# Where tiles lie in memory: gaps ahead of the feed-forward and turned-output tiles of a four-layer decoder trunk

## The chip, the cores and the metric

The kernel runs on one core of a Trainium2 chip. The core has five engines that run side by side, each with its own queue of instructions: TensorE (PE; its weight loads are shown apart as PEld), VectorE (DVE), ScalarE (ACT), GpSimd (POOL) and SyncE (SP), which here only issues DMAs. Data that the engines work on lies in a memory of 128 partitions, the same byte range in every partition; "byte 182784" below is an address within a partition. TensorE multiplies a stationary operand, which a weight load brings into the array, by a moving operand, which streams past it.

The metric is the time of one execution on the device, in microseconds, as the median of several runs.

## The reference

A decoder trunk of four layers on 256 positions of width 1024, in float32. Each layer is a token mixer and a feed-forward block, each followed by a layer norm of `ALPHA * x + h`. Layers 0 and 3 mix with HGRN2 (a gated linear recurrence), layer 1 with mLSTM, layer 2 with an S5 state space.

```python
for i in range(DEPTH):
    kind = i % N_MIXERS
    if kind == 0:
        h = _hgrn2_mixer(x, ...)
    elif kind == 1:
        h = _mlstm_mixer(x, ...)
    else:
        h = _s5_mixer(x, ...)
    x = _layernorm(ALPHA * x + h, ln_g[i, 0], ln_b[i, 0])
    x = _layernorm(ALPHA * x + _swiglu(x, ffn_w_gate_up[i], ffn_w_down[i]), ln_g[i, 1], ln_b[i, 1])

def _swiglu(x, w_gate_up, w_down):
    gate, up = jnp.split(x @ w_gate_up, 2, axis=-1)
    return (jax.nn.silu(gate) * up) @ w_down
```

The hidden width of the feed-forward block is 2816. The HGRN and mLSTM mixers end with a product of the mixed values and a 1024 x 1024 weight.

## The kernel before

**Products of split numbers.** TensorE multiplies operands of type float32r, whose mantissa is short. So that the result is as exact as float32, each operand is split in two: `hi` is the value rounded to float32r (ScalarE, line 151), `lo` is what is left (VectorE, line 152). A product is then three matmuls, hi by hi, lo by hi and hi by lo (`mm3`, lines 182 to 184, and for the last block of a layer the loop of line 374). `ws_wide` (lines 212 and 215) does the same with two matmuls for 512 and 256 columns.

**Weights.** All weights come from HBM in pieces of 1 MB (128 partitions of 2048 floats), in the order of one list that `plan` makes. SP issues the loads, three stage buffers ahead; ScalarE and VectorE split each piece into `hi` and `lo` tiles of 1024 floats, of which there are eight each. All of these, and the activations `xx`, lie at multiples of 512 bytes.

**The feed-forward block** (`ffn`, line 299) walks over 11 blocks of 256 hidden columns. For blocks 2 to 9, `across` computes gate and up with the weights as the stationary operand (64 matmuls a block, lines 212 and 215), adds the parts into `sum` tiles, applies silu, multiplies, and splits the result into `hh` and `hl` (`parts`, lines 344 and 345). Blocks 0, 1 and 10 are computed the other way round and turned (line 339) before they are split. `dproj` then adds the block's share of the down projection: here `hh` and `hl` are the stationary operands, 128 columns at a time, and the moving operands are 512 columns of the split down weights. A block's `dproj` is 2 halves of the block x 2 halves of the positions x 2 halves of the output x 3 = 24 matmuls. In the steady part of a layer, `across` of one block and `dproj` of the one before follow each other.

**The output projection** (`out_proj`) of the HGRN and mLSTM layers works in the same way: `transposed` allocates two tiles `oh` and `ol` of 8192 bytes for the turned and split output of the mixer; these are the stationary operands, and the moving ones are the split weights. It is 96 matmuls of 512 columns a layer, or four times 24.

**S5 preparation.** VectorE work for layer 2's tables is spread over the feed-forward blocks of layers 0 and 1.

**Where tiles lie.** Tiles come from pools. A pool's tiles are laid one behind the other in the order of their first allocation, and a pool is put behind those that are open at that time; when it closes, the next one takes its place. A tile that comes to lie on an older one waits until the older one is released (`reuse_waits="tile"`). So the size of a tile that is never used shifts all tiles of the pool that follow it. The kernel before does this at three places: `GAPS` (line 33) gives the bytes of a tile `gap` which `ffn` allocates ahead of all others (lines 304 to 306); one column of it is set by a memset on POOL, so that the allocation has a writer. Layer 3 has no such tile.

The tiles of `ffn` are 1024 bytes each (`sg`, `hd`, `hh`, `hl`, `sum`) and those of `transposed` 8192, so all tiles of one kind and layer have the same offset past a multiple of 512. Before the change this is:

| tiles | pool position where the gap or tile starts | gap, bytes | first tile behind it | offset past a multiple of 512 |
|---|---|---|---|---|
| `ffn`, layer 0 | 182752 | 32 | 182784 | 0 |
| `ffn`, layer 1 | 181568 | 256 | 181824 | 64 |
| `ffn`, layer 2 | 145600 | 448 | 146048 | 128 |
| `ffn`, layer 3 | 145600 | none | 145600 | 192 |
| `oh`, `ol`, layers 0 and 3 | 153280 | none | 153280 | 192 |
| `oh`, `ol`, layer 1 | 149696 | none | 149696 | 192 |

In the HGRN layers the pool also holds the mask and three score tiles `att` ahead of `oh`, and behind it `v`, the gates `g`, and in a second pool behind the first the keys, queries and decay tiles of the score loop (lines 640 to 700). In the mLSTM layer nearly all of its tiles lie behind `ol`.

Of the kernel before, what the change touches and what calls it, by code (L numbers as in the profile page):

```python
# [9 lines left out]
F32 = mybir.dt.float32  # L10
# [7 lines left out]
P = 128  # L18
# [11 lines left out]
BIG = 1e30  # L30
AHEAD = 1
ROWS = (0, 1, NBLK - 1)
GAPS = (32, 256, 448)


class Trunk:
# [262 lines left out]
    def ffn(self, i, gb, out=None, perm=False, rev=False, extra=()):  # L299
        nc, tc = self.nc, self.tc  # L300
        with tc.tile_pool(name=self.uid("ffn"), bufs=2, reuse_waits="tile") as fp:
            down = [[self.bank("a") for _ in range(2)] for _ in range(2)]

            if i < len(GAPS):
                gap = fp.tile([P, GAPS[i] // 4], F32, name=self.uid("gap"), bufs=1)
                nc.gpsimd.memset(gap[:, 0:1], 0.0)
            hid, gu, dn, turned, wide = {}, {}, {}, {}, {}
            self.table("silu_and_others")
            extra = list(extra)
# [114 lines left out]
            for h in range(2):  # L424
                self.layernorm(h, down[h], gb, out, perm, rev)

    def transposed(self, pool):

        return tuple(pool.tile([P, KD, S], F32R, name=self.uid(n)) for n in ("oh", "ol"))

    def out_proj(self, key, gb, ot, turn):
# [934 lines left out]
def plan(layers, ffn):  # L1366

    p = []
    for i in layers:
        j = i // 3  # L1370
        if i % 3 == 0:
            p += [("w_hg", j, s) for s in (0, 1, 8, 9, 10, 11, 4, 5, 6, 7, 2, 3, 12, 13, 14, 15)] + [("w_ho", j, s) for s in range(4)]
        elif i % 3 == 1:
            p += [("w_ml", s) for s in range(4)] + [("ml_gw",)] + [("w_ml", s) for s in range(4, 12)] + [("w_mo", s) for s in range(4)]
        else:
            p += [("w_si", s) for s in range(4)] + [("w_so", s) for s in (0, 1, 2, 4, 5, 3, 6, 7)]
        if ffn:
            gu = lambda b: [("w_gu", i, b, 0), ("w_gu", i, b, 1)]
            dn = lambda b: [("w_dn", i, b)]
            p += gu(0) + gu(1) + dn(0)  # L1380
            for b in range(2, NBLK):
                p += gu(b) + dn(b - 1)
            p += dn(NBLK - 1)
    return p


def trunk(tc, aps, out, layers=range(DEPTH), ffn=True):
    with ExitStack() as ctx:
        t = Trunk(ctx, tc, aps)
        nc = tc.nc  # L1390
        layers = list(layers)
        t.plan = plan(layers, ffn)
        with tc.tile_pool(name="first", bufs=1, reuse_waits="tile") as fp:
            t.warm_up(fp)
# [127 lines left out]
```

## Time and profile before

| | |
|---|---|
| median of 3 runs | 1251.75 us (1250.62 to 1251.87) |
| profiled execution | 1251.88 us |
| its span, first to last instruction | 1250.1 us |
| mean granted TensorE clock | 0.997 |
| HBM read | 233.94 MB |

The profile is of one execution. It gives each engine's busy time, the groups of instructions by line with their mean durations, the waits, and the order of time. Two things help in reading it here. A matmul's duration in a row (some 390 ns for 512 columns) is longer than the distance to the next matmul, because one begins while the one before still drains; so a rate is read from the time of many matmuls in a row, not from the mean duration. And rows name tiles as out<-in, moving operand first: `a<-hi,hh` is a matmul into bank `a` that moves `hi` past the stationary `hh`.

### The profile page before, as it was taken

To read this page: it belongs to the slowest core of one execution; us is meant where nothing else is said; L and a number is where in the kernel's file an instruction comes from. 1 tells how busy PE (TensorE), PEld (TensorE's weight loads), DVE (VectorE), ACT (ScalarE), POOL (GpSimd) and SP (SyncE) were. 2 spreads that over 40 slices of the span, in tenths; PEclk is the share of its full clock that TensorE was granted. 3 is DMA by queue.
4 is the path that set the end of the run, shared out by engine and by line. 5 is a ranking of instruction groups with operands and counts; after the bars stand their busy time and mean duration, and the time that the engine had idled before them with its cause. 6 is when DMAs were issued, how large, how long until landed. Compare 5 with 4: busy or idle time off the path is not lost.

```text
span 1250.1 us, 21400 instructions
## 1 busy us (share of the span) xinstructions
PE 1230.6 (98%) x8464; PEld 1031.6 (83%) x8464; DVE 956.2 (76%) x1717; ACT 694.3 (56%) x1126; POOL 34.8 (3%) x63
## 2 busy tenths in 40 slices
PE   9999999999999999999999999999999999999997
PEld 8977888888798888888877788888889878888886
DVE  6887889796887799887699696666486887766664
ACT  7755575565477555555544355555359654555551
POOL 0000000000100000000000000000000000000000
PEclk9999999999999999999999999999999999999999
DMA  8733476666373288667565456555446432755540
GB/s 325 290 137 135 150 267 236 219 220 225 121 274 129 102 305 307 234 235 247 209 217 210 165 202 231 191 181 201 169 173 219 157 134 102 270 184 186 194 143 34
DMA packets 50245, 247.91 MB, mean 198 GB/s; under 512 B 6337, under 2 KB 15953, under 8 KB 23777
## 3 DMA queue, kind: packets, MB, share of 16 engines
q1 hardware_dynamic: 50016, 246.46, 55.0%
q8 instruction: 66, 1.08, 0.3%
q14 instruction: 35, 0.28, 0.1%
q0 software_dynamic: 128, 0.09, 0.0%
HBM read 233.94 MB, written 12.58 MB: 197 GB/s over the span
## 4 chain that ended last, share of the span: by engine, by line
PE 88%; DVE 6%; DMA 2%; ACT 2%; issue 1%; POOL 0%; SPq 0%; DVEq 0%; ACTq 0%; POOLq 0%
PE g L212 18%; PE g L182 10%; PE g L184 10%; PE g L183 9%; PE g L215 9%; PE a L183 8%; PE a L182 8%; PE a L184 8%; DVE lo L152 2%; PE a L374 1%; PE t L273 1%; DMA bc<-in_s_bc 1%; PE a L668 1%; DMA w<-in_w_gu 1%; PE a L548 1%
## 5 line engine op out<-in xcount | busy, mean ns | idle before, releaser
L152 DVE TENSOR_TENSOR lo<-w,hi 128x1024 fp32r<-128x1024 f32 x388 | 470.3, 1219 | 117.6 <-ACT hi L151 107.6
L151 ACT CAST hi<-w 128x1024 fp32r<-128x1024 f32 x388 | 405.3, 1051 | 186.5 <-PE a L183 98.0
L212 PE MATMUL g<-xx,hi 128*128 128x512 f32 x1024 | 356.6, 397 | 0.5 <-DVE sum L356 0.4
L215 PE MATMUL g<-xx,lo 128*128 128x256 f32 x1024 | 264.6, 279 | 0.0
L212 PEld LDWEIGHTS g<-xx,hi 128*128 128x128 f32 x1024 | 185.8, 188 | 37.5 <-DVE sum L356 1.2
L215 PEld LDWEIGHTS g<-xx,lo 128*128 128x128 f32 x1024 | 193.0, 188 | 10.8
L182 PE MATMUL g<-hi,xx 128*128 128x512 f32 (+1 forms) x416 | 166.5, 401 | 2.4 <-ACT xx L292 2.1
L184 PE MATMUL g<-lo,xx 128*128 128x512 f32 (+1 forms) x416 | 163.7, 395 | 0.0
L183 PE MATMUL g<-hi,xx 128*128 128x512 f32 (+1 forms) x416 | 163.4, 394 | 0.0
L183 PE MATMUL a<-hi,hl 128*128 128x512 f32 x328 | 129.3, 394 | 1.0 <-DVE hl L345 1.0
L182 PE MATMUL a<-hi,hh 128*128 128x512 f32 x328 | 129.0, 394 | 0.1
L184 PE MATMUL a<-lo,hh 128*128 128x512 f32 x328 | 129.0, 393 | 0.0
L355 ACT COPY sum<-g 128x256 f32<-128x256 f32 x128 | 47.7, 373 | 139.7 <-PE g L212 139.5
L356 DVE TENSOR_TENSOR sum<-g,sum 128x256 f32<-128x256 f32 x128 | 53.9, 421 | 61.9 <-ACT sum L355 61.5
L182 PEld LDWEIGHTS g<-hi,xx 128*128 128x128 f32 x416 | 78.4, 189 | 19.3 <-ACT xx L292 3.5
L184 PEld LDWEIGHTS g<-lo,xx 128*128 128x128 f32 x416 | 78.2, 188 | 16.4 <-DVE lo L152 0.4
L183 PEld LDWEIGHTS g<-hi,xx 128*128 128x128 f32 x416 | 78.4, 188 | 14.6
L183 PEld LDWEIGHTS a<-hi,hl 128*128 128x128 f32 x328 | 61.6, 188 | 15.6 <-DVE hl L345 1.8
L184 PEld LDWEIGHTS a<-lo,hh 128*128 128x128 f32 x328 | 61.6, 188 | 13.6
L182 PEld LDWEIGHTS a<-hi,hh 128*128 128x128 f32 x328 | 61.5, 188 | 13.3 <-ACT hh L344 0.9
L182 PE MATMUL g<-xx,hi 128*128 128x256 f32 x192 | 54.5, 284 | 0.0
L184 PE MATMUL g<-xx,hi 128*128 128x256 f32 x192 | 54.4, 283 | 0.0
(308 smaller groups left out, 1734.9 us busy)
## 6 DMA issues: line engine op xcount, KB each, us to landing
w<-in_w_gu SPq DMA_DIRECT2D x88, 1024.0 KB
w<-in_w_dn SPq DMA_DIRECT2D x44, 1024.0 KB
w<-in_w_hg SPq DMA_DIRECT2D x30, 1024.0 KB
w<-in_w_ml SPq DMA_DIRECT2D x12, 1024.0 KB
gb<-in_ln SPq DMA_DIRECT2D x8, 1024.0 KB
w<-in_w_ho SPq DMA_DIRECT2D x8, 1024.0 KB
w<-in_w_so SPq DMA_DIRECT2D x8, 1024.0 KB
w<-in_w_mo SPq DMA_DIRECT2D x4, 1024.0 KB
```

What stands on the lines that cost most here:

```text
L151: self.nc.scalar.copy(hi, x)
L152: i = self.nc.vector.tensor_tensor(lo, x, hi.bitcast(F32), ALU.subtract).ins
L182: mm(ps, lh, rh, start=start, stop=False)
L183: mm(ps, ll, rh, start=False, stop=False)
L184: mm(ps, lh, rl, start=False, stop=stop)
L212: whole = lambda: mm(ps, hi[:, c], self.xx[:, k].rearrange("p i t -> p (i t)"), start=k == 0, stop=k == KD - 1)
L215: mm(ps[:, S:], lo[:, c], self.xh[:, k], start=False, stop=False)
L273: nc.tensor.transpose(pt[:, (k % 4) * P : (k % 4 + 1) * P], z[:, k * P : (k + 1) * P], self.ident)
L355: nc.scalar.copy(t, ps[:, S:])
L356: nc.vector.tensor_tensor(t, ps[:, 0:S], t, ALU.add)
L374: nc.tensor.matmul(down[h][n], hidden(h, j, b)[x], dn[j][b][y][:, f], start=False, stop=(x, y, b) == steps[-1])
L548: nc.tensor.matmul(o, att[:, 2 * h + hd % 2, :], v[:, h, c], start=True, stop=h == 0)
```

## The change

The gap becomes a helper of its own. Each of the four feed-forward layers calls it with its own size, and `transposed` calls it with 320 bytes ahead of `oh`.

```diff
-GAPS = (32, 256, 448)
+GAPS = (32, 192, 320, 320)
...
-            if i < len(GAPS):
-                gap = fp.tile([P, GAPS[i] // 4], F32, name=self.uid("gap"), bufs=1)
-                nc.gpsimd.memset(gap[:, 0:1], 0.0)
+            self.gap(fp, GAPS[i])
...
+    def gap(self, pool, size):
+
+        t = pool.tile([P, size // 4], F32, name=self.uid("gap"), bufs=1)
+        self.nc.gpsimd.memset(t[:, 0:1], 0.0)
+
     def transposed(self, pool):
 
+        self.gap(pool, 320)
         return tuple(pool.tile([P, KD, S], F32R, name=self.uid(n)) for n in ("oh", "ol"))
```

With the pool positions of the table above: 181568 + 192 = 181760 = 355 x 512; 145600 + 320 = 145920 = 285 x 512 (layers 2 and 3); 153280 + 320 = 153600 = 300 x 512; 149696 + 320 = 150016 = 293 x 512. Layer 0's feed-forward tiles stay where they are. In the HGRN and mLSTM layers everything behind `oh` moves by 320 bytes too. There are four more memsets on POOL than before, one in layer 3's `ffn` and three in `transposed`.

## The prediction

> **What bounds the kernel now.** I read the page first, then the view of windows, then the order of time where a window had to be cut. Of the page these rows matter:
>
> ```profile
> span 1250.1 us, 21400 instructions
> ...
> PE 1230.6 (98%) x8464; PEld 1031.6 (83%) x8464; DVE 956.2 (76%) x1717; ACT 694.3 (56%) x1126; POOL 34.8 (3%) x63
> ...
> PEclk9999999999999999999999999999999999999999
> ...
> PE 88%; DVE 6%; DMA 2%; ACT 2%; issue 1%; POOL 0%; SPq 0%; DVEq 0%; ACTq 0%; POOLq 0%
> ```
>
> TensorE is busy for 98% of the span, at a granted clock of nine tenths or more in every slice, and 88% of the chain that ended last is TensorE. A busy TensorE need not run at its best rate, though, and the change alters no instruction of it: it can only help if matmuls follow one another more closely. So I looked at the middles of the four feed-forward layers (columns: stretch, its length, then busy time and number of instructions for PE, PEld, DVE, ACT and POOL, the granted clock, the DMA share and GB/s):
>
> ```profile
> 200.00:300.00 100.00, 100.00 (x571) 85.26 (x570) 84.47 (x149) 58.02 (x98) 0.00 (x0) 1.00 0.68 234
> 485.00:600.00 115.00, 115.00 (x649) 97.33 (x648) 91.40 (x155) 65.71 (x110) 0.33 (x4) 1.00 0.71 248
> 775.00:890.00 115.00, 115.00 (x607) 97.72 (x606) 72.19 (x96) 60.09 (x95) 0.00 (x0) 1.00 0.52 186
> 1100.00:1215.00 115.00, 115.00 (x610) 98.32 (x609) 72.49 (x96) 60.28 (x96) 0.00 (x0) 1.00 0.52 183
> ```
>
> In each of them TensorE has no idle time at all, and its clock is 1.00. There the end is set by the distance from one matmul to the next and by nothing else.
>
> **The same work at four offsets.** The four feed-forward layers run the same program, but before the change their tiles `hh` and `hl` (the stationary operands of the down projection) begin at 0, 64, 128 and 192 bytes past a multiple of 512, in the order of the layers; the turned outputs `oh` and `ol` begin at 192 in all three layers that have them. The moving operands, the split weights, begin at 0 everywhere. The trace of before thus holds the experiment already. For one down-projection block of each layer I cut a window from the start of its first matmul to the start of the first matmul behind it, and a fifth one for a part of the output projection of layer 1. Each holds 24 matmuls of 512 columns (24 weight loads; PE counts 25, as the tail of the one before reaches in):
>
> ```profile
> 217.35:222.79 5.44, 5.44 (x25) 4.50 (x24) 5.44 (x12) 2.71 (x5) 0.00 (x0) 1.00 0.58 200
> 515.33:520.93 5.60, 5.60 (x25) 4.49 (x24) 3.90 (x6) 2.81 (x5) 0.00 (x0) 1.00 0.70 227
> 806.41:812.00 5.59, 5.59 (x25) 4.51 (x24) 3.65 (x6) 2.80 (x5) 0.00 (x0) 1.00 0.57 189
> 1131.15:1136.64 5.49, 5.49 (x25) 4.51 (x24) 3.65 (x6) 2.81 (x5) 0.00 (x0) 1.00 0.52 185
> 416.84:422.34 5.50, 5.50 (x25) 4.46 (x24) 4.71 (x8) 3.08 (x4) 0.00 (x0) 1.00 0.55 194
> ```
>
> Divided by 24: 226.7 ns a matmul at offset 0 (layer 0), 233.3 at 64 (layer 1), 232.9 at 128 (layer 2), 228.8 at 192 (layer 3), and 229.2 for the turned output, which also lies at 192. The last two agree although they belong to different stages: that speaks for the offset and against something else that differs between layers. The cuts were read from the order of time; for layer 0 it shows
>
> ```profile
> 217.35 0.39 PE L182 MATMUL a<-hi,hh 128*128 128x512 f32 x1
> ...
> 222.56 0.39 PE L184 MATMUL a<-lo,hh 128*128 128x512 f32 x1
> 222.79 0.39 PE L212 MATMUL g<-xx,hi 128*128 128x512 f32 x1
> ```
>
> Does a shorter block shorten the layer, or does the next wait take it back? From one block's start to the next block's start:
>
> ```profile
> 217.35:233.97 16.62, 16.62 (x89) 14.25 (x88) 15.21 (x25) 8.85 (x14) 0.00 (x0) 1.00 0.62 193
> 515.33:532.09 16.76, 16.76 (x90) 14.23 (x88) 10.77 (x15) 8.82 (x14) 0.00 (x0) 1.00 0.78 258
> 806.41:823.20 16.79, 16.79 (x90) 14.25 (x89) 10.57 (x15) 8.83 (x14) 0.00 (x0) 1.00 0.55 187
> 1131.15:1147.83 16.68, 16.68 (x90) 14.26 (x88) 10.57 (x15) 8.83 (x14) 0.00 (x0) 1.00 0.53 189
> ```
>
> Take the block off and 11.18, 11.16, 11.20 and 11.19 us remain: the rest of the period is alike in all four. What a block gains, its layer gains.
>
> **The change part by part.** It moves tiles and adds four one-column memsets on POOL (one in layer 3's feed-forward, three ahead of the turned outputs); no matmul, copy or DMA is added or taken away. How many matmuls are affected is in the groups:
>
> ```profile
> L183 PE MATMUL a<-hi,hl 128*128 128x512 f32 x328 | 129.3, 394 | 1.0 <-DVE hl L345 1.0
> L182 PE MATMUL a<-hi,hh 128*128 128x512 f32 x328 | 129.0, 394 | 0.1
> L184 PE MATMUL a<-lo,hh 128*128 128x512 f32 x328 | 129.0, 393 | 0.0
> ...
> L182 PE MATMUL g<-hi,oh 128*128 128x512 f32 x48 | 18.6, 397 | 0.0
> ...
> L374 PE MATMUL a<-lo,hh 128*128 128x512 f32 x24 | 7.7, 397 | 0.0
> ```
>
> Three rows of 328 and three like the last (line 374, 24 each) make 1056 matmuls, 264 a layer, or 11 blocks of 24. The turned outputs have six rows of 48, 288 matmuls, or 12 blocks of 24. With 5.44 us for every block at offset 0:
> - layer 0: its gap stays, nothing.
> - layer 1: 11 x (5.60 - 5.44) = 1.76 us.
> - layer 2: 11 x (5.59 - 5.44) = 1.65 us.
> - layer 3: 11 x (5.49 - 5.44) = 0.55 us.
> - output projections: 12 x (5.50 - 5.44) = 0.72 us.
>
> The sum is 4.68 us. What is late next is TensorE again: layer 0 keeps its 16.62 us period with VectorE busy for 15.21 of it, while in layers 1 to 3 VectorE has at most 10.77, so nothing in those layers stands ready to take the gain back.
>
> The memsets: POOL already has three like them, the second at
>
> ```profile
> 432.81 0.72 POOL L225 TENSOR_TENSOR rs<-rs,odds 128x1 f32<-128x1 f32 x1 [17.96 <-DVE rs L224]
> 433.49 0.09 POOL L306 MEMSET gap<- 128x1 f32 x1
> ```
>
> 0.09 us each. What stands behind one on POOL is the next layernorm's power (line 225) or, in the mixers, a memset or the head norm, which come microseconds later: POOL's own idle time, 97% of the span, hides it. With the cover gone, four would cost 0.36 us. A memset waits until the tiles that lay there are released; each new one lies over tiles that a neighbour in the same pool has to wait for too, so I cost this wait at nothing.
>
> Everything behind the gap in the same pool moves as well: in the HGRN layers `v`, the gates and the score tiles go from 192 to 0, in the mLSTM layer all tiles behind its `oh` by 320. Operands that move together keep their distance. One pair does not: `att` stays at 192 and `v` goes to 0.
>
> ```profile
> L548 PE MATMUL a<-v,att 128*128 128x128 f32 x64 | 10.0, 278 | 0.0
> ```
>
> These 64 are a quarter as wide; with the largest step seen above, 6.6 ns, up or down on each, that is 0.4 us to either side. I take nothing and keep both ends. For VectorE's and ScalarE's own work at offset 0 the nearest rows are line 360, three operands on one offset, in layer 0 (offset 0) and in layer 3 (192):
>
> ```profile
> L360 DVE TENSOR_TENSOR sum<-sum,sum 128x256 f32<-128x256 f32 x12 | 4.9, 412 | 0.2
> ...
> L360 DVE TENSOR_TENSOR sum<-sum,sum 128x256 f32<-128x256 f32 x13 | 5.5, 425 | 0.4
> ```
>
> 412 against 425 ns: no slower at 0, and off the path in any case. I take zero.
>
> The profiled execution took 1251.88 us, 1.78 around the span of 1250.1; it is 0.13 over the median of 1251.75. 1251.88 - 4.68 is **1247.2 us**, and from the median it would be 1247.1. I keep 1247.2, which is 0.36% faster; about 0.2% (2.5 us) is what a measurement of this kernel can tell from no change.
>
> [...]
>
> **The rivals.**
> 1. *No change, about 1251.8 us.* The rate belongs to the layer, not to the offset, or the tiles don't come to lie where the sums of the gaps say. The four layers differ in more than offset: layers 0 and 1 carry the S5 preparation, DMA shares run from 0.52 to 0.71. Against it: layers 2 and 3 have the same load (72.19 and 72.49 us of VectorE, DMA 0.52 both) and still differ by 4 ns a matmul, and layers 0 and 1 share the extra load and differ most.
> 2. *Partly taken back, about 1249.0.* VectorE is the second engine: 91.40 of 115 us in layer 1. If it or the weights' DMAs (0.78 in that layer's period) set the pace as soon as TensorE is quicker, layer 1's 1.76 us go, and 1251.88 - 2.92 is left. Against it: layer 0 holds the quick rate with VectorE at 84.47 of 100.
> 3. *Slower.* The place is the score loop of the two HGRN layers, where all operands now share offset 0:
>
> ```profile
> L640 DVE TENSOR_TENSOR q<-q,f 128x256 f32<-128x256 f32 (+2 forms) x56 | 24.4, 436 | 0.0
> ...
> L640 DVE TENSOR_TENSOR k<-k,f 128x256 f32<-128x256 f32 (+1 forms) x48 | 18.9, 397 | 0.3
> ```
>
> If VectorE's reads of three tiles at offset 0 collided, these 43.3 us would grow, and the matmuls there wait for them. To end 2.5 us above before it must lose 4.68 + 2.5 = 7.2 us, so these instructions must grow by 17% if all of it reaches the path; at a fifth the time would be 1251.88 - 4.68 + 8.7 = 1255.9. Line 360 speaks against it: 3% less at offset 0, not 17% more.
>
> **How the numbers follow.** My forecast 0.80 at 1247.2; no change 0.09; partly taken back 0.06; slower 0.05. The forecast's own range: the sum goes from 4.68 - 0.36 - 0.4 = 3.9 to 4.68 + 0.4 = 5.1 us, so 1246.8 to 1248.0, and the three runs of before, which spread over 1.25 us, add 0.6 to either side: 1246.2 to 1248.6. Taking in the second rival, which has 1249.0 and the same spread, the upper end is 1249.6, and 14 in 100 are left out above; the lower end I put at 1246.0. Faster by over 0.2% means under 1249.25: the forecast and two thirds of the second rival, 0.84. Within 0.2%: the rest of that rival and the first, 0.11. Slower 0.05.
>
> **What would show it.** In the changed kernel's windows of 24 matmuls layers 1 to 3 and the output projections should show 5.44 us, and the periods 16.62 to 16.64; layer 0 should be unchanged. If blocks shorten and periods don't, rival 2 is right; if blocks stay at 5.60, 5.59 and 5.49, rival 1 is. Longer means on line 640, and idle time of TensorE near 50 to 112 and 970 to 1032 us, would show rival 3. The forecast is wrong if the blocks at offset 0 are not alike in all layers.

## The result, and the profile after

| | before | after |
|---|---|---|
| median | 1251.66 us (1249.41 to 1253.03, 6 runs) | 1246.78 us (1245.20 to 1247.08, 6 runs) |
| ratio, 95% interval | | 0.9961 (0.9948 to 0.9974) |
| profiled execution, its span | 1251.88, 1250.1 us | 1247.08, 1245.3 us |

The kernel became 0.39% faster, 4.9 us by the medians; the interval allows 3.3 to 6.5 us. The forecast was 1247.2.

The page after differs little in its sums: the matmuls are as many and TensorE is busy for 98% again, but for 4.2 us less. Of the page of the changed kernel:

```profile
PE 1226.4 (98%) x8464; PEld 1031.3 (83%) x8464; DVE 956.4 (77%) x1717; ACT 694.8 (56%) x1126; POOL 35.0 (3%) x67
```

The view of windows, cut as in the prediction, shows the cause. One down-projection block of layers 0 to 3, and the same part of the output projection of layer 1 (stretch, its length, then busy time and count of PE, PEld, DVE, ACT, POOL, the granted clock, the DMA share, GB/s):

```profile
234.49:239.94 5.45, 5.45 (x26) 4.50 (x24) 2.47 (x5) 1.73 (x3) 0.00 (x0) 1.00 1.01 403
532.31:537.75 5.44, 5.44 (x25) 4.50 (x24) 3.70 (x6) 2.80 (x5) 0.00 (x0) 1.00 0.50 185
819.99:825.44 5.45, 5.45 (x26) 4.50 (x24) 3.70 (x6) 2.81 (x5) 0.00 (x0) 1.00 0.52 180
1143.40:1148.84 5.44, 5.44 (x25) 4.50 (x24) 3.69 (x6) 2.81 (x5) 0.00 (x0) 1.00 0.51 179
417.38:422.82 5.44, 5.44 (x25) 4.46 (x24) 4.74 (x8) 3.08 (x4) 0.00 (x0) 1.00 0.54 194
```

All 24 matmuls now take 5.44 us wherever they stand (5.45 is the rounding of the cut), where layers 1 to 3 and the output projection had 5.60, 5.59, 5.49 and 5.50. From block to block, in layers 1 and 2:

```profile
515.69:532.31 16.62, 16.62 (x89) 14.25 (x88) 10.57 (x15) 8.85 (x14) 0.00 (x0) 1.00 0.76 257
803.37:819.99 16.62, 16.62 (x89) 14.25 (x88) 10.56 (x15) 8.84 (x14) 0.00 (x0) 1.00 0.53 194
```

The periods were 16.76 and 16.79; layer 0 always had 16.62. Every block's gain is a period's gain.

Where the 4.8 us between the two spans came from is read by cutting both executions at the first turn (line 273) of a layer norm. In before, the stretches that hold layer 1's feed-forward block, the S5 mixer, and the feed-forward blocks of layers 2 and 3 are

```profile
434.20:625.76 191.56, 191.56 (x1022) 159.97 (x1023) 156.58 (x290) 106.36 (x173) 3.38 (x11) 1.00 0.72 252
625.76:725.67 99.91, 92.87 (x1241) 75.16 (x1241) 85.34 (x118) 42.27 (x56) 1.48 (x3) 0.98 0.53 191
725.67:914.85 189.18, 188.16 (x951) 157.29 (x952) 125.70 (x182) 97.76 (x152) 1.47 (x3) 1.00 0.53 189
1050.46:1250.10 199.64, 192.18 (x974) 161.79 (x974) 130.96 (x188) 94.32 (x149) 1.71 (x2) 0.99 0.47 169
```

and after

```profile
434.64:625.08 190.44, 190.32 (x1022) 159.81 (x1023) 156.52 (x290) 106.64 (x173) 3.39 (x11) 1.00 0.72 254
625.08:723.38 98.30, 92.28 (x1242) 75.10 (x1241) 85.32 (x118) 42.30 (x56) 1.48 (x3) 0.98 0.55 195
723.38:910.71 187.33, 186.50 (x951) 157.21 (x952) 125.70 (x182) 97.92 (x152) 1.47 (x3) 1.00 0.53 191
1046.20:1245.27 199.07, 191.60 (x974) 161.73 (x974) 130.96 (x188) 94.39 (x149) 1.71 (x2) 0.99 0.47 169
```

That is 1.12, 1.61, 1.85 and 0.57 us less. The second of these is a surprise: the S5 mixer has no tile that the change moves. It is taken up behind the experiments.

### The profile page after: what moved, and what is told of

The parts are those of the page before. It is cut to its first block, busy times and chain, and to the rows that moved or that the text cites. A ratio compares the mean times of both kernels' runs of the same rounds, so it can differ in the third digit from the quotient of the medians.

```text
span 1245.3 us, 21404 instructions
## 1 busy us (share of the span) xinstructions
PE 1226.4 (98%) x8464; PEld 1031.3 (83%) x8464; DVE 956.4 (77%) x1717; ACT 694.8 (56%) x1126; POOL 35.0 (3%) x67
## 4 chain that ended last, share of the span: by engine, by line
PE 87%; DVE 7%; DMA 3%; ACT 2%; issue 1%; POOL 0%; SPq 0%; DVEq 0%; ACTq 0%; POOLq 0%
PE g L212 18%; PE g L182 10%; PE g L184 9%; PE g L183 9%; PE g L215 9%; PE a L183 8%; PE a L182 8%; PE a L184 8%; DVE lo L152 2%; PE a L372 1%; DMA w<-in_w_dn 1%; PE t L273 1%; DMA bc<-in_s_bc 1%; PE a L672 1%; DMA w<-in_w_gu 1%
```

## The experiments

The theory: the distance between matmuls of 512 columns is set by where the stationary tile lies against the moving one. The rivals: the rate belongs to the layer and its load; the tiles that move along with the outputs gain or lose something of their own; each operand's own distance from a multiple of 512 counts.

### Each half of the change alone

Feed-forward gaps without those ahead of the turned outputs:

```diff
     def transposed(self, pool):
 
-        self.gap(pool, 320)
```

> The feed-forward gaps of the change, but none ahead of the turned outputs, which stay at 192. Theory (the offset of the stationary tile sets the distance between matmuls): blocks of 24 take 5.44 us in all four layers, parts of the output projections still 5.50; 3.96 us under the kernel before, about 1247.7. Rival (the rate belongs to the layer, and the change gained elsewhere): blocks at 5.60, 5.59 and 5.49 in layers 1 to 3, about 1251.7.

Measured: 1247.18 us, ratio 0.9957 (0.9943 to 0.9972). Its windows of layers 1 and 2, and of the output projection:

```profile
532.11:537.55 5.44, 5.44 (x25) 4.50 (x24) 3.69 (x6) 2.81 (x5) 0.00 (x0) 1.00 0.52 184
820.33:825.78 5.45, 5.45 (x26) 4.51 (x25) 3.69 (x6) 2.82 (x5) 0.00 (x0) 1.00 0.48 176
416.20:421.70 5.50, 5.50 (x25) 4.46 (x24) 4.72 (x8) 3.08 (x4) 0.00 (x0) 1.00 0.54 194
```

The feed-forward blocks are quick, the output projection stays at 5.50: as the theory has it. In time this half alone can't be told from the whole change.

The other half alone:

```diff
-GAPS = (32, 192, 320, 320)
+GAPS = (32, 256, 448, 0)
...
-            self.gap(fp, GAPS[i])
+            if GAPS[i]:
+                self.gap(fp, GAPS[i])
```

> The gaps ahead of the turned outputs alone; the feed-forward gaps as before (none in layer 3). Theory: parts of the output projections 5.44 us, feed-forward blocks 5.44, 5.60, 5.59 and 5.49 as before; 0.72 us under the kernel before, about 1250.9, too little to time well. Rival (what moves behind the turned outputs costs in the score loops): not under the kernel before, and the HGRN stages longer by more than 0.3 us each.

Measured: 1250.36 us, ratio 0.9994 (0.9983 to 1.0005): no difference that the runs could tell, which agrees with 0.72 us and with nothing. Of the rival's two stages, cut at the first turn of the layer norm behind each, the first HGRN stage took 134.94 us against 134.42 before, the second 135.53 against 135.61. The half microsecond of the first is not owed to the tiles behind the outputs: with these put back (the next kernel) it was 135.01 us, and with these moved it was also 134.43 (the first kernel under "Other offsets"). Layer 1's block and its output projection:

```profile
533.75:539.35 5.60, 5.60 (x25) 4.51 (x24) 3.69 (x6) 2.80 (x5) 0.00 (x0) 1.00 0.54 186
...
417.58:423.02 5.44, 5.44 (x25) 4.46 (x24) 4.74 (x8) 3.08 (x4) 0.00 (x0) 1.00 0.56 196
```

The two have changed places against the kernel above. The rate goes with the tile and not with the layer.

### The tiles behind the turned outputs

```diff
-        return tuple(pool.tile([P, KD, S], F32R, name=self.uid(n)) for n in ("oh", "ol"))
+        ot = tuple(pool.tile([P, KD, S], F32R, name=self.uid(n)) for n in ("oh", "ol"))
+        self.gap(pool, 192)
+        return ot
```

> The change with a further gap of 192 bytes behind the turned outputs, so that the outputs lie at 0 and all that follows them at its old offset. Theory: as after, about 1246.8. Rival (the tiles that follow gain or lose by the move): off from after by more than 1 us, in the HGRN and mLSTM stages.

Measured: 1247.24 us, ratio 0.9958 (0.9943 to 0.9973), 0.5 us from after. The tiles that move along cost and gain nothing that can be seen. The groups of the changed kernel say the same of the score loops, which the prediction's third rival feared for; the costlier of them kept its 436 ns:

```profile
L644 DVE TENSOR_TENSOR q<-q,f 128x256 f32<-128x256 f32 (+2 forms) x56 | 24.4, 436 | 0.0
```

### The other way: everything at 64

```diff
-GAPS = (32, 192, 320, 320)
+GAPS = (96, 256, 384, 384)
...
-        self.gap(pool, 320)
+        self.gap(pool, 384)
```

> All four feed-forward layers and all three turned outputs at 64 past a multiple of 512. Theory: every block 5.60 us, layer 0 too; over after by 44 x 0.16 + 12 x 0.16 = 8.96 us, about 1255.7. Rival (the rate belongs to the layer): layer 0 stays at 5.44, and the time is near that of before.

Measured: 1253.85 us, ratio 1.0017 (1.0008 to 1.0027): 0.56% or 7.0 us over after by the two ratios, where 8.96 were expected. Layer 0, which no kernel above had touched, and the output projection:

```profile
234.77:240.37 5.60, 5.60 (x26) 4.51 (x24) 2.47 (x5) 1.73 (x3) 0.00 (x0) 1.00 1.01 407
...
418.58:424.18 5.60, 5.60 (x26) 4.46 (x25) 4.71 (x8) 3.07 (x4) 0.00 (x0) 1.00 0.55 190
```

The rival "the rate belongs to the layer" falls here: layer 0 slowed down like the others. Part of the missing 2 us is in the output projections, below.

### Other offsets

Three kernels put each layer at another offset. In the first:

```diff
-GAPS = (32, 192, 320, 320)
+GAPS = (288, 512, 704, 768)
```

> Feed-forward layers 0 to 3 at offsets 256, 320, 384 and 448. If the pattern repeats every 256 bytes: blocks of 24 at 5.44, 5.60, 5.59 and 5.49 us. If only whole multiples of 512 are quick: layer 0 above 5.44. If the rate belongs to the layer: 5.44 in all, as after.

Windows of layers 0 to 3 (offsets 256, 320, 384, 448):

```profile
234.10:239.54 5.44, 5.44 (x25) 4.51 (x24) 2.47 (x5) 1.73 (x3) 0.00 (x0) 1.00 0.99 383
533.45:539.04 5.59, 5.59 (x25) 4.51 (x24) 3.69 (x6) 2.80 (x5) 0.00 (x0) 1.00 0.58 192
821.68:827.27 5.59, 5.59 (x25) 4.50 (x24) 3.65 (x6) 2.81 (x5) 0.00 (x0) 1.00 0.51 183
1146.29:1151.78 5.49, 5.49 (x25) 4.51 (x24) 3.65 (x6) 2.80 (x5) 0.00 (x0) 1.00 0.52 190
```

These are, to 0.01 us, the figures of before at 0, 64, 128 and 192. At these four offsets the pattern repeats after 256 bytes; 512 is more than is needed. The second and third:

```diff
-GAPS = (32, 192, 320, 320)
+GAPS = (64, 384, 416, 384)
```

> Feed-forward layers 0 to 3 at offsets 32, 192, 96 and 64: two offsets known from before in other layers (192 was layer 3, 64 was layer 1), and two that are new. Theory: layer 1 at 5.49 us, layer 3 at 5.60, layers 0 and 2 at 5.44 to 5.60. Rival (the layer's load): layers 0, 1 and 3 keep 5.44 as after.

Offsets 32, 192, 96 and 64 in layers 0 to 3:

```profile
234.54:240.14 5.60, 5.60 (x25) 4.51 (x24) 2.47 (x5) 1.73 (x3) 0.00 (x0) 1.00 0.97 388
533.21:538.70 5.49, 5.49 (x25) 4.51 (x24) 3.66 (x6) 2.80 (x5) 0.00 (x0) 1.00 0.55 185
822.39:828.01 5.62, 5.62 (x25) 4.52 (x24) 3.65 (x6) 2.81 (x5) 0.00 (x0) 1.00 0.52 197
1147.82:1153.42 5.60, 5.60 (x26) 4.51 (x24) 3.70 (x6) 2.81 (x5) 0.00 (x0) 1.00 0.48 173
```

```diff
-GAPS = (32, 192, 320, 320)
+GAPS = (192, 416, 352, 576)
```

> Feed-forward layers 0 to 3 at offsets 160, 224, 32 and 256: two new offsets, and two that other layers had in the earlier sweeps (32 in layer 0, 256 in layer 0). Theory (the distance between the two operands, repeating every 256 bytes): layer 2 as layer 0 had at 32, 233.4 ns a matmul, layer 3 at 226.8; 160 and 224 somewhere from 226 to 234. Rival (the layer): layers 2 and 3 both off from these by more than 1 ns.

Offsets 160, 224, 32 and 256:

```profile
235.47:241.06 5.59, 5.59 (x25) 4.50 (x24) 2.42 (x5) 1.73 (x3) 0.00 (x0) 1.00 1.01 416
534.22:539.82 5.60, 5.60 (x25) 4.50 (x24) 3.70 (x6) 2.81 (x5) 0.00 (x0) 1.00 0.56 193
822.23:827.84 5.61, 5.61 (x26) 4.51 (x25) 3.69 (x6) 2.82 (x5) 0.00 (x0) 1.00 0.55 174
1146.77:1152.21 5.44, 5.44 (x25) 4.51 (x24) 3.69 (x6) 2.81 (x5) 0.00 (x0) 1.00 0.52 173
```

An offset gives the same figure in whichever layer it stands (192 in layers 1 and 3, 64 in layers 1 and 3, 32 in layers 0 and 2, 256 in layers 0 and 3), to 0.01 us. The 5.62 at 96 lies just above the range expected. A block of 24, by offset past a multiple of 256:

| offset | 0 | 32 | 64 | 96 | 128 | 160 | 192 | 224 |
|---|---|---|---|---|---|---|---|---|
| us | 5.44 | 5.60 | 5.60 | 5.62 | 5.59 | 5.59 | 5.49 | 5.60 |

Only 0 is quick, 192 is nearly so, and the rest lie 3% above, with no slope between them. No offset beats 0, so no version beyond the change follows. In time the three kernels ran once each: 1250.34 and 1252.57 us beside 1252.85 of before, and 1250.43 beside 1250.11. Single runs can't settle a few microseconds here, as 19 runs of the kernel before lie between 1248.20 and 1253.39 us; the windows decide.

### One operand against the other

All tiles of the change moved down by 64 bytes, weights and activations with them:

```diff
-        odds = c.tile([P, 96], F32, name="odds")
+        odds = c.tile([P, 80], F32, name="odds")
```

> All tiles of the change 64 bytes lower, the weights and the activations too: stationary and moving operands all at 448, none moved against the other. If the distance between the two operands' offsets counts: blocks at 5.44 us and 1246.8 in all, as after. If each operand's own distance from a multiple of 512 counts: all matmuls of 512 columns slower by up to 6 ns, some 3600 of them with a stationary operand that moved: up to 20 us more.

Measured: 1249.75 us in one run, beside 1252.85 of before: 3.1 us less, where the change had 4.9, which one run can't tell apart. The block of layer 1:

```profile
534.49:539.93 5.44, 5.44 (x25) 4.51 (x24) 3.69 (x6) 2.81 (x5) 0.00 (x0) 1.00 0.54 188
```

Both operands lie at 448 here and the block is as quick as with both at 0, where `hh` and `hl` at 448 against weights at 0 had 5.49; the other three layers show 5.44 or 5.45 too. What counts is the one's place against the other; being "at a multiple of 512" is merely a way to get it. That is shown for operands in the same place; that a distance other than 0 costs the same wherever the pair lies was not tried.

The activations alone at 448 (a gap of 64 bytes behind them holds the rest in place):

```diff
-        odds = c.tile([P, 96], F32, name="odds")
+        odds = c.tile([P, 80], F32, name="odds")
...
+        self.gap(c, 64)
         self.ident = c.tile([P, P], F32, name="ident")
```

> The activations xx alone at 448, all else as after. Where xx is the stationary operand (the projections into the mixers, feed-forward blocks 0, 1 and 10) the distance is 448 - 0, where it is the moving one (the middle of the feed-forward layers) it is 0 - 448. Theory: both kinds get slower than the 227 and 233 + 116 ns of after, the first by the step of offset 448; the down projections keep 5.44. Rival (only tiles freshly written by ScalarE and VectorE at another offset are slow): no change.

Measured: 1250.03 us in one run, beside 1252.85 of before. Two windows of this kernel, 24 matmuls of 512 columns with `xx` stationary (layer 2's last feed-forward block) and 288 of 256 columns with `xx` moving (the gates of the first HGRN layer):

```profile
894.41:899.90 5.49, 5.49 (x25) 4.51 (x24) 1.23 (x1) 1.03 (x1) 0.00 (x0) 1.00 0.64 234
17.11:51.12 34.01, 34.01 (x290) 33.88 (x288) 25.88 (x28) 30.10 (x42) 0.00 (x0) 1.00 0.86 316
```

and the same two after the change:

```profile
891.94:897.38 5.44, 5.44 (x25) 4.50 (x24) 1.23 (x1) 1.03 (x1) 0.00 (x0) 1.00 0.60 229
17.18:51.83 34.65, 34.65 (x290) 34.51 (x288) 25.93 (x28) 30.25 (x42) 0.00 (x0) 1.00 0.85 314
```

With `xx` stationary it went from 5.44 to 5.49, the figure of offset 192 (448 less 256) again. The rival that only freshly written tiles are slow falls: `xx` was written by the layer norm some 150 us ahead of this window. With `xx` as the moving operand there are two cases. In the middle of the feed-forward layers, which the expectation names, the 64 matmuls between two down projections (32 of 512 columns and 32 of 256, in turn) took in layer 1 of this kernel

```profile
537.65:548.91 11.26, 11.26 (x66) 9.80 (x64) 8.48 (x16) 6.03 (x10) 0.00 (x0) 1.00 0.91 331
```

and after the change

```profile
537.75:548.94 11.19, 11.19 (x66) 9.74 (x64) 8.41 (x15) 6.04 (x10) 0.00 (x0) 1.00 0.89 332
```

They got slower, as expected, but by 2 ns for a pair, not by the 6.6 ns that `hh` at 64 costs each matmul. Where matmuls of 256 columns follow one another they got quicker, 118.1 against 120.3 ns in the windows above; in the mLSTM layer 68 of them took 7.71 us against 8.15. So the rule of offsets is shown for runs of 512-column matmuls that move weights past `hh`, `hl`, the turned outputs or `xx`. It does not cover all matmuls of 512 columns: those that move `xx` stand 233 ns apart after the change (the 233 of the expectation), although both operands lie at 0. What sets the distance there, and for 256 columns, was not looked into.

## Why the prediction was right, and where it was not

**Rates.** 226.7, 233.3, 232.9 and 228.8 ns at offsets 0, 64, 128 and 192 held in every kernel to 0.01 us a block of 24, and 5.44 us came out in all changed blocks. That the offset and not the layer sets them was argued from one trace; the kernels with offsets exchanged show it. Why the distance between two operands should matter the traces don't show: the weight loads of a feed-forward block were busy for 4.49 to 4.52 us at every offset.

**Layers 2 and 3.** 1.65 and 0.55 us were predicted; their stretches shrank by 1.85 and 0.57. For layer 3 the other kernels agree: 199.65 us with the slow blocks (gaps ahead of the turned outputs alone) and 199.03 with quick ones (feed-forward gaps only, and tiles behind put back). Layer 2's stretch scatters: the same three had 187.80, 186.27 and 186.27 us, where before had 189.18 and after 187.33. That 1.85 lies so near to 1.65 is partly chance. At offset 64 layer 3's last stretch was 200.9 us, 1.8 over the 199.07 after, where 1.76 belongs to it.

**Layer 1.** 1.76 predicted, 1.12 measured between these two executions, though each block gained its 0.16. The stretch scatters by itself: with the same quick blocks it was 191.3 us in the kernel with feed-forward gaps only and 190.2 with the tiles behind put back. What varies was not followed further; the S5 preparation's waits lie in it.

**Output projections: the mis-sized term.** The prediction took 12 blocks of 24 at 0.06 us, 0.72 in all. The three projections, from their first matmul to the last, were in before

```profile
116.85:141.42 24.57, 24.55 (x116) 19.27 (x114) 17.90 (x35) 9.39 (x13) 3.41 (x5) 1.00 0.21 77
416.84:441.20 24.36, 24.35 (x113) 19.39 (x112) 18.59 (x34) 11.66 (x16) 0.77 (x2) 1.00 0.35 122
1032.91:1057.44 24.53, 24.52 (x115) 19.25 (x114) 17.85 (x33) 9.42 (x13) 2.57 (x3) 1.00 0.21 75
```

and after

```profile
117.21:141.71 24.50, 24.43 (x115) 19.25 (x114) 17.89 (x35) 9.40 (x13) 3.41 (x5) 1.00 0.21 78
417.38:441.64 24.26, 24.20 (x114) 19.39 (x112) 18.61 (x34) 11.66 (x16) 0.77 (x2) 1.00 0.33 121
1028.70:1053.20 24.50, 24.45 (x115) 19.25 (x114) 17.88 (x33) 9.41 (x13) 2.62 (x4) 1.00 0.20 76
```

0.07 + 0.10 + 0.03 = 0.20 us. Of the 96 matmuls 26 stand behind the first turn of the layer norm (line 273), and these got no quicker: from that turn to the end of the projection it was 7.00, 7.00 and 6.98 us before and 6.98, 7.00 and 7.00 after. VectorE, which has the layer norm to do, is busy for all of these stretches (7.00, 7.00 and 6.98 us before; 6.98, 7.00 and 7.00 after), so its chain may well be what ends last there; no run shows it. The 70 ahead of the turn did get quicker, by 0.08, 0.13 and 0.09 us, but the turn took back 0.04 of it each time. In the order of time of before, in layer 3:

```profile
1049.30 0.48 DVE L268 SCALAR_TENSOR_TENSOR x<-x,mv,gb 128x256 f32<-128x256 f32 x1
...
1049.83 0.88 DVE L269 SCALAR_TENSOR_TENSOR x<-x,rs,gb 128x256 f32<-128x256 f32 x2
...
1050.06 0.39 PE L182 MATMUL a<-hi,oh 128*128 128x512 f32 x1
...
1050.46 0.41 PE L273 MATMUL t<-ident,x 128*128 128x128 f32 x2
```

The turn at 1050.46 stands in TensorE's order and waits for the normed `x`, whose first part VectorE ended at 1050.31 (1049.83 and 0.48); it starts 0.40 us behind the matmul ahead of it here and 0.44 after the change, so a quicker stream waits longer ahead of it. The reverse is seen at offset 64, where that distance is 0.31 us: by 96 x 6.6 ns each projection should be 0.63 us over after, and the three took 24.70, 24.61 and 24.67, only 0.20, 0.35 and 0.17 more. So "the matmuls are the path", read in the middle of the feed-forward layers, was carried over to a place where a quicker matmul is passed on in part only: 0.20 of the 0.72 us.

**POOL's memsets.** Hidden, as costed: 0.09 to 0.12 us each, none with an instruction waiting behind it that was due.

**The S5 stretch, 1.61 us that the change did not earn.** TensorE at half clock in before and its idle time just ahead, and then the same eight matmuls after; columns as above, the clock is the third number from the end:

```profile
692.60:696.00 3.40, 3.40 (x10) 2.60 (x8) 3.40 (x4) 0.48 (x1) 0.00 (x0) 0.51 0.11 12
690.30:692.30 2.00, 0.03 (x1) 0.03 (x1) 1.97 (x2) 2.00 (x3) 0.00 (x0) 1.00 0.00 0
```

```profile
691.90:694.00 2.10, 2.10 (x10) 1.50 (x8) 2.10 (x3) 0.47 (x1) 0.00 (x0) 1.00 0.00 0
```

In before TensorE stood idle for 2.0 us, as ScalarE came late to the `xx` that it needs, having waited 1.73 us for a weight piece, and the clock then was 0.51 for 3.40 us: the eight matmuls took 1.30 us more than after. The execution after has such a drop too, elsewhere in its S5 stretch:

```profile
655.70:659.10 3.40, 3.40 (x68) 2.99 (x67) 3.40 (x6) 0.66 (x2) 0.00 (x0) 0.50 0.96 333
```

That one cost nothing that can be seen: its stretch is as long (98.30 us) as that of a kernel without any drop (98.29, below). So what differs is where the drop falls. It is no effect of the change: the S5 mixer's tiles lie where they lay, and two kernels that differ in tiles of other stages alone fall on both sides, the one with feed-forward gaps only at 99.90 us with the half clock at 691.70, the one with the tiles behind put back at 98.29 without:

```profile
624.88:724.78 99.90, 92.18 (x1241) 74.79 (x1241) 85.43 (x118) 42.13 (x56) 1.48 (x3) 0.98 0.53 192
691.70:695.10 3.40, 3.40 (x9) 2.65 (x8) 3.40 (x4) 0.47 (x1) 0.00 (x0) 0.50 0.08 10
```

So the difference of the two spans, 4.8 us, agrees with the sum of 4.68 partly by luck. 1.12 + 1.85 + 0.57 in the feed-forward stretches and 0.20 in the projections, which overlap a little with them, make some 3.7 us of the change's own, known no better than the microsecond or so by which the stretches of layers 1 and 2 scatter; 1.6 came from the S5 stretch, 1.3 of it in the eight matmuls at half clock, and about half a microsecond went the other way ahead of layer 1, where the first HGRN stage alone scatters by as much. The interval of the timed runs, 3.3 to 6.5 us, holds both sums.

**The rivals.** No change: falls by the exchanged offsets. Partly taken back by VectorE: did not happen in the steady part, since the periods of layers 1 and 2 are 16.62 like layer 0's; what was taken back was in the output projections instead. Slower by the score loops: their row is unchanged, and TensorE was busy for 61.89 and 61.88 of the 62 us from 50 to 112 and from 970 to 1032, as before (61.88 and 61.85). The same 24 matmuls, at a granted clock of 1.00 each time, took 5.44 us with the stationary tile at 0 and 5.62 at 96.

## What to carry to other kernels

Where TensorE runs without idle time and float32r matmuls of 512 columns follow one another and make the pace, let stationary and moving tiles start at the same place modulo 256 bytes; here that was worth up to 3% of those that move weights (5.44 us for 24 of them, against up to 5.62), for a few hundred bytes of padding. Look for such a thing by cutting windows around equal runs of matmuls in different stages: the page's mean over all four layers blurs it (394 ns a matmul before, 391 after). Before summing a gain over all instructions of a kind, ask for each stage whether they are its path.

## What the runs showed that was not expected

- The pattern is not one of alignment but of distance, has a period of 256 bytes as far as tried, and is nearly flat: 5.44 us at 0, 5.49 at 192, 5.59 to 5.62 everywhere else that was tried (steps of 32).
- Other matmuls behave otherwise: those of 256 columns in a row went from 120.3 to 118.1 ns with the moving tile 64 bytes lower, and those of 512 columns that move `xx` stand 233 ns apart with both tiles at 0.
- The granted clock fell to half for 3.40 us in the S5 stretch of some executions: to 0.51 in before, behind 2.0 us in which TensorE stood idle, and there the stretch took 1.6 us more than after; to 0.50 in after, behind 1.8 us without a matmul, and there it cost nothing that can be seen. In the kernel with the tiles behind put back the clock was 1.00 over the whole stretch. What makes it fall no run here tested.
